# Gated MLP in seven-product units: GeLU of the chunk before issued behind a PSUM copy, and the opening's weight split, column sums and copies in another order

## The chip, the cores and the metric

The kernel runs on one core of one Trainium2 chip. The metric is the device time of one execution in microseconds, the median of several. TensorE (PE) multiplies, VectorE (DVE) and ScalarE (ACT) work elementwise, GpSimd (POOL) and SyncE (SP) here mostly issue DMAs. Each engine works through its own instructions in the order in which the kernel writes them and waits on semaphores for the others.

## What is computed

Two decoder layers on 512 tokens of 1024 channels. Each ends in the same gated MLP, and that is the part that the change touches:

```python
def conv_ffn(x, norm, w_up, dw_w, dw_b, w_down):
    h = rms_norm(x, norm) @ w_up                          # 1024 -> 2 * 3072
    g = causal_dwconv(h[..., :D_FF], dw_w, dw_b)          # width 3 over tokens
    u = h[..., D_FF:]
    return (jax.nn.gelu(g) * u) @ w_down                  # 3072 -> 1024
```

Around it, in both layers, stand a token mixer and a cross-attention, each with RMSNorm and a residual sum. All matrix products are made in three passes: each operand is split into a rounded high part and the rest, and `mm3` (lines 184 to 188) multiplies high by high, high by low and low by high into one PSUM bank. So each weight block needs a high part (an ACT copy) and a low part (a DVE subtraction).

## The kernel before

Activations lie with channels on the 128 partitions and tokens along the row. `ffn` (line 835) cuts the 3072 gate and 3072 value channels into 24 chunks of 128 each. Chunks 0 and 1 are plain: eight k-steps of 128x512 products. Chunks 2 to 23 are **units**: a 2 by 2 block product of half the k-range and half the tokens (256), done in seven products instead of eight, as in the schemes of Strassen and Winograd. The token side of the sums (`seven.T1` to `T4`) is made once for a layer by `Seven.sums`. The weight side (`Blocks`) is made for each unit: the raw blocks are loaded, `high` (line 798) copies a block on ACT (L815), `low` (line 820) subtracts on DVE (L822), and `low` of a11, s3 and s2 also issues accumulating DMAs on POOL's queue (L825, L828, L830), which turn the raw block into the next sum. The sums hang on each other: a11 must be split before s3 can be made, s3 before s1 and s2, and s2 before s4.

`unit(c)` (line 927) has three PSUM tiles of 128x256: G, F and H. G is the left half of the gate. F begins as a copy of the first product in G (L924 in `ahead`, which is called for the next unit before a unit ends) and then takes the products s2, s3 and a22. It is copied out after s2 (L941, into the left half of tile u) and after s3 (L955). s3 may not be added before L941 has read F. H takes s1 and s4. PE's order in a unit is: s1 into H, s2 into F, a12 into G, s3 into F; then the down projection, or in units 2 and 3 a plain chunk; then a11 of the next unit, s4 into H and a22 into F.

The down projection follows four chunks behind: unit c, from 4 on, has a `Down` that copies two 128x512 rows of the residual X into PSUM (`bank`, L854, ACT), adds 24 products of 128x512 onto each pair, and copies them home (L858).

The elementwise work on a finished unit is the generator `gating(c, ...)` (line 897). It is held in `left` and stepped by `next(left)` inside the following unit. Its steps in order: the token convolution (L891 on ACT, two taps L894 on DVE), the GeLU (L896, ACT), the product with the values (L910, DVE), the high part of the result (L913, ACT) and its low part (L915, DVE). In `unit` the GeLU step stands ahead of L941, L910 behind it, then the copy of the next unit's a22 (L815), then L913, and then the two `bank` copies.

`opening()` (line 1044) starts the MLP of a layer. PE makes the two products of plain chunk 0 (`start(0)` and `start(1)`, 24 products each) and in their midst `mean_of` (L287, L288), the column sums of squares. From these come the root (L1056), the loading of the GeLU table (L1057) and the reciprocal `norm.r` (L1059), with which chunk 0's gate is scaled (L1012). Then follow its convolution, GeLU and value (L891, L894, L896, L1015, L1018, L1020 on DVE and ACT), mixed with splits of weights for units 2 (`first`) and 3 (`second`) and with `ahead(first)`.

What sets the order: `tc.manual_schedule(engines=ORDERED)` keeps PE, ACT, DVE and POOL in the order of the code. SP's loads are placed by the scheduler, and they wait for free buffers; the raw weights have three.

## Time and profile before

| | |
|---|---|
| median of 3 runs | 1452.84 us (1452.17 to 1453.44) |
| the profiled execution | 1449.17 us, its span 1447.4 us |
| PE busy | 1423.2 us, 98% of the span |
| DVE, ACT busy | 1077.3 us (74%), 912.8 us (63%) |
| granted TensorE clock, mean | 0.996 |
| MLP units, layer 0 and layer 1 | first L941 at 380.0 us, last L941 at 1403.6 us, 44 in all |

The profiled execution is the one whose rows are quoted; it was 3.67 us below the median of the other three. A row of the timeline has the start in the span, the duration, the engine, the line and operation, the tile written and those read, the size, and in brackets how long the engine had idled before and which instruction ended that wait. Matmuls are pipelined, so their durations overlap: their cost is the distance between two starts. With PE at 98% nearly all that can be won or lost is in the places where PE's starts stand further apart than usual.

### The profile page before, as it was taken

What the parts mean: (1) busy time and instruction counts of PE and PEld (TensorE: products, weight loads), DVE (VectorE), ACT (ScalarE), POOL (GpSimd) and SP (SyncE); (2) the same over time, 40 slices, a digit from 0 to 9 for tenths busy, and PEclk for the clock granted to TensorE, in tenths of its full rate; (3) what the DMA queues carried; (4) which work ended last, traced back from release to release, by engine and by line L of the source; (5) the groups of instructions that cost most, each with busy time, mean ns of one, the idle gap of its engine ahead of it and who ended that gap; (6) DMA issues with size and microseconds to landing.
All of it is one profiled execution on the core that took longest, in us unless ns stands there. A gap on an engine that the chain in (4) does not pass through costs nothing.

```text
span 1447.4 us, 22826 instructions
## 1 busy us (share of the span) xinstructions
PE 1423.2 (98%) x8650; PEld 1265.9 (87%) x8650; DVE 1077.3 (74%) x1792; ACT 912.8 (63%) x1600; POOL 316.8 (22%) x333
## 2 busy tenths in 40 slices
PE   9999999999899999999999999999989999999998
PEld 8888888987799999999988777899869999999997
DVE  7987775769676676666788997877777676676665
ACT  7668754667466666666665547667655666666664
POOL 0012300100122222222008992011012222222211
PEclk9999999999999999999999999999999999999999
DMA  8522232543577777777442364345347777777751
GB/s 305 188 88 88 90 129 75 123 108 118 122 170 174 162 175 172 163 172 167 129 131 88 117 170 147 99 96 132 105 112 168 168 176 166 166 174 171 162 125 59
DMA packets 80030, 204.32 MB, mean 141 GB/s; under 512 B 9008, under 2 KB 9520, under 8 KB 79920
## 3 DMA queue, kind: packets, MB, share of 16 engines
q1 hardware_dynamic: 50832, 150.15, 33.7%
q0 software_dynamic: 28800, 52.44, 21.2%
q8 instruction: 67, 1.10, 0.3%
q14 instruction: 43, 0.35, 0.1%
q10 hardware_dynamic: 288, 0.27, 0.1%
HBM read 145.16 MB, written 2.10 MB: 102 GB/s over the span
## 4 chain that ended last, share of the span: by engine, by line
PE 84%; DVE 6%; issue 3%; ACT 2%; DMA 2%; POOL 2%; SPq 0%; POOLq 0%; DVEq 0%; ACTq 0%
PE mm L186 20%; PE mm L187 20%; PE mm L188 20%; PE aux L186 7%; PE aux L187 7%; PE aux L188 7%; PE mm L458 2%; DMA raw<-in_wv 1%; DVE wlo L167 1%; DMA raw<-raw 1%; POOL actf L1484 1%; DVE wlo L203 0%; PE aux L532 0%; ACT whi L166 0%; POOL act L167 0%
## 5 line engine op out<-in xcount | busy, mean ns | idle before, releaser
L187 PE MATMUL mm<-act,whi 128*128 128x512 f32 (+2 forms) x1029 | 357.7, 348 | 0.5 <-DVE act L181 0.4
L186 PE MATMUL mm<-act,whi 128*128 128x512 f32 (+2 forms) x1029 | 357.5, 348 | 0.0
L188 PE MATMUL mm<-act,wlo 128*128 128x512 f32 (+2 forms) x1029 | 357.3, 347 | 0.0
L187 PEld LDWEIGHTS mm<-act,whi 128*128 128x128 f32 x1029 | 195.3, 190 | 26.5 <-DVE act L167 1.0
L186 PEld LDWEIGHTS mm<-act,whi 128*128 128x128 f32 x1029 | 195.1, 190 | 26.5 <-ACT tmp L1483 0.8
L188 PEld LDWEIGHTS mm<-act,wlo 128*128 128x128 f32 x1029 | 195.3, 190 | 23.9 <-DVE wlo L167 0.6
L186 PE MATMUL mm<-bigr,bigr 128*128 128x256 f32 x704 | 201.1, 286 | 9.8 <-ACT tmp L941 6.6
L187 PE MATMUL mm<-bigr,bigr 128*128 128x256 f32 x704 | 200.3, 285 | 0.0
L188 PE MATMUL mm<-bigr,bigr 128*128 128x256 f32 x704 | 200.3, 285 | 0.0
L186 PE MATMUL aux<-act,whi 128*128 128x512 f32 x431 | 168.6, 391 | 0.0
L187 PE MATMUL aux<-act,whi 128*128 128x512 f32 x431 | 168.2, 390 | 0.0
L188 PE MATMUL aux<-act,wlo 128*128 128x512 f32 x431 | 167.7, 389 | 0.0
L166 ACT ACTIVATE whi<-raw 128x1024 fp32r<-128x1024 f32 (+1 forms) x95 | 96.5, 1020 | 84.7 <-PE mm L187 44.0
L828 POOL DMA_DIRECT2D raw<-wa x100 | 87.1, 890 | 284.6 <-DVE bigr L822 166.4
L186 PEld LDWEIGHTS mm<-bigr,bigr 128*128 128x128 f32 x704 | 136.2, 193 | 11.0 <-ACT tmp L941 7.4
L171 DVE TENSOR_TENSOR tmp<-mm,tmp 128x256 f32<-128x256 f32 x130 | 53.9, 419 | 121.2 <-PE mm L188 118.6
L815 ACT ACTIVATE bigr<-raw 128x512 fp32r<-128x512 f32 x176 | 109.0, 622 | 53.4 <-DVE wlo L203 42.2
L187 PEld LDWEIGHTS mm<-bigr,bigr 128*128 128x128 f32 x704 | 136.3, 194 | 0.0
L188 PEld LDWEIGHTS mm<-bigr,bigr 128*128 128x128 f32 x704 | 136.3, 194 | 0.0
L822 DVE TENSOR_TENSOR bigr<-raw,bigr 128x512 fp32r<-128x512 f32 x176 | 120.9, 688 | 13.4 <-ACT bigr L815 9.6
L825 POOL DMA_DIRECT2D raw<-raw x50 | 43.2, 865 | 399.4 <-DVE wlo L822 205.6
L167 DVE TENSOR_TENSOR wlo<-raw,whi 128x1024 fp32r<-128x1024 f32 (+1 forms) x75 | 90.3, 1209 | 21.0 <-ACT whi L166 20.7
(354 smaller groups left out, 3084.9 us busy)
## 6 DMA issues: line engine op xcount, KB each, us to landing
raw<-wa POOLq DMA_DIRECT2D x150, 256.0 KB, 3.9
wa<-in_wpair SPq DMA_DIRECT2D x88, 256.0 KB, 3.7
raw<-in_wpair SPq DMA_DIRECT2D x44, 512.0 KB, 3.8
big<-in_wdown SPq DMA_DIRECT2D x42, 512.0 KB, 4.0
raw<-raw POOLq DMA_DIRECT2D x50, 256.0 KB, 4.9
raw<-in_pw SPq DMA_DIRECT2D x24, 512.0 KB, 3.3
raw<-in_win SPq DMA_DIRECT2D x20, 512.0 KB, 3.3
raw<-in_wk SPq DMA_DIRECT2D x16, 512.0 KB, 3.4
```

Source lines behind the costliest of these rows:

```text
L166: A.activation(hi, src, AF.Copy)
L167: fetched[1] = (eng or V).tensor_tensor(lo, src, hi.bitcast(F32), op=ALU.subtract)
L171: V.tensor_tensor(out, a, b, op=ALU.add)
L186: PE.matmul(ps, wh, xh, start=first, stop=False, skip_group_check=onto)
L187: PE.matmul(ps, wh, xl, start=False, stop=False, skip_group_check=onto)
L188: PE.matmul(ps, wl, xh, start=False, stop=last, skip_group_check=onto)
L458: PE.matmul(p, m[j], x, start=k == 0 and j == 0 and x is hi, stop=k == C - 1 and x is lo)
L815: A.activation(self.w[name][0], self.block(name), AF.Copy)
L822: V.tensor_tensor(lo, self.block(name), hi.bitcast(F32), op=ALU.subtract)
L825: G.dma_start(self.r, self.z, accum_op=ALU.add)
L828: G.dma_start(block, self.a22, accum_op=ALU.add)
L1484: G.tensor_tensor(z[:, s:], z[:, s:], f[:, s:], op=ALU.add)
```

## The change

Two edits. In `unit`, the step that issues the GeLU of the chunk before now stands behind the copy L941. In `opening`, the column sums come later on PE (after all of `start(0)` and two k-steps of `start(1)`), block a11 of unit 3 is loaded and split ahead of the last sums of the norm, `ahead(first)` comes before the second and third step of chunk 0's gate, block s3 of unit 3 is split in the opening too (before, it was split in unit 2), and s4 of unit 2 one step later.

```diff
@@ unit
             m(c, F, "s2", seven.T2, False)
-            next(left, None)
             u, f, g = tmp_f(), tmp_f(), tmp_f()
             A.activation(u[:, :M], F, AF.Copy)
+            next(left, None)
             next(left, None)
             high(c + 1, "a22")
@@ opening
             ss = split(norm.ss)
-            start(0, range(6))
+            start(0)
+            start(1, range(2))
             mean = mean_of(ss)
-            start(0, range(6, C))
-            start(1)
+            start(1, range(2, C))
             Norm.due = None
+            pairs[second].load()
+            pairs[second].load_second()
+            both(second, "a11")
             for _ in seven.sums(3):
                 pass
...
             fetch(2)
-            pairs[second].load()
-            pairs[second].load_second()
             g = gate(0)
             next(g)
             w[-1].low()
-            both(first, "s4")
+            pairs[second + 1].load()
+            chains = ahead(first)
+            both(second, "s3")
             next(g)
             next(g)
-            both(second, "a11")
+            both(first, "s4")
             next(g, None)
-            pairs[second + 1].load()
-            chains = ahead(first)
             left = values(0)
```

On ACT, in a unit with a down projection (here unit 5 of layer 0), this stood in a row before. L896 is the GeLU, L941 the copy of F, L815 a weight block's high part, L913 the high part of the gated chunk, L854 the two bank copies:

```order
L891 ACTIVATE tmp_4212<-tmp_4074,par 128x512
L815 ACTIVATE bigr_4227<-raw_3971 128x512
L896 ACTIVATE tmp_4212<-tmp_4212 128x512
L941 ACTIVATE tmp_4248<-mm_4171 128x256
L815 ACTIVATE bigr_4253<-wa_4152 128x512
L913 ACTIVATE act_4267<-tmp_4212 128x512
L854 ACTIVATE aux_4270<-x 128x512
```

And now, where the copy has the line number 940:

```order
L891 ACTIVATE tmp_4212<-tmp_4073,par 128x512
L815 ACTIVATE bigr_4227<-raw_3971 128x512
L940 ACTIVATE tmp_4247<-mm_4171 128x256
L896 ACTIVATE tmp_4212<-tmp_4212 128x512
L815 ACTIVATE bigr_4253<-wa_4152 128x512
L913 ACTIVATE act_4267<-tmp_4212 128x512
L854 ACTIVATE aux_4270<-x 128x512
```

The GeLU moved behind the copy, which waits for PE's s2 products; L913 and L854 stay behind the GeLU.

On ACT in the opening of layer 0, from the split of a plain weight (L200) to the first L941, before. L815 here are: s4 of unit 2 (`raw_3040`), a11 of unit 3 (`whi` from `raw_3648`), s3 of unit 3 (`bigr` from `raw_3648`):

```order
L200 ACTIVATE whi_3645<-raw_3643 128x1024
L891 ACTIVATE tmp_3656<-tmp_3654,par 128x512
L815 ACTIVATE bigr_3659<-raw_3040 128x512
L896 ACTIVATE tmp_3656<-tmp_3656 128x512
L815 ACTIVATE whi_3665<-raw_3648 128x512
L924 ACTIVATE mm_3674<-mm_3673 128x256
L815 ACTIVATE bigr_3701<-raw_3648 128x512
L1020 ACTIVATE act_3704<-tmp_3656 128x512
L941 ACTIVATE tmp_3723<-mm_3674 128x256
```

And now; a11 of unit 3 is no longer among them, as it stands ahead of the root, right behind the split of the sums of squares:

```order
L200 ACTIVATE whi_3656<-raw_3654 128x1024
L891 ACTIVATE tmp_3661<-tmp_3659,par 128x512
L924 ACTIVATE mm_3667<-mm_3666 128x256
L815 ACTIVATE bigr_3681<-raw_3619 128x512
L896 ACTIVATE tmp_3661<-tmp_3661 128x512
L815 ACTIVATE bigr_3689<-raw_3040 128x512
L1020 ACTIVATE act_3707<-tmp_3661 128x512
L940 ACTIVATE tmp_3722<-mm_3667 128x256
```

L924 moved up by three places, s3 of unit 3 from behind L924 and the GeLU to between them; L1020 still stands ahead of the copy of F.

## The prediction

> **What bounds the kernel now.** I read the page first, and in it the busy times:

> ```profile
> PE 1423.2 (98%) x8650; PEld 1265.9 (87%) x8650; DVE 1077.3 (74%) x1792; ACT 912.8 (63%) x1600; POOL 316.8 (22%) x333
> ```

> PE is busy for 98% of the span, so the time lies in PE's starts, and any wait of PE is lost. Then the view of waits, for PE alone; its columns are the total, the times and the longest:

> ```profile
> PE mm L186 <- ACT tmp L941: 6.6, 4, 2.6
> PE stat L287 <- ACT act L166: 4.0, 2, 2.9
> PE mm L186 <- ACT mm L924: 3.2, 2, 2.4
> ```

> These three, all within the MLP, are what the change is aimed at: the column sums and the first copies of F in the two openings, and two later copies L941. They occur eight times in 44 units. So an ordinary unit has no wait on PE at all. The timeline of PE in the opening of layer 0:

> ```profile
> 358.43 0.39 PE L188 MATMUL mm<-act,wlo 128*128 128x512 f32 x1
> ...
> 359.89 0.51 PE L287 MATMUL stat<-act,ones 128*128 128x512 f32 x1 [1.07 <-ACT act L166]
> ...
> 370.55 0.28 PE L188 MATMUL mm<-bigr,bigr 128*128 128x256 f32 x1
> 373.23 0.58 PE L186 MATMUL mm<-bigr,bigr 128*128 128x256 f32 x1 [2.40 <-ACT mm L924]
> ...
> 377.57 0.28 PE L188 MATMUL mm<-act,wlo 128*128 128x256 f32 x1
> 380.37 0.58 PE L186 MATMUL mm<-bigr,bigr 128*128 128x256 f32 x1 [2.52 <-ACT tmp L941]
> ```

> The view of windows gives the granted clock behind a wait (its columns: length, PE busy, clock, DMA share, GB/s):

> ```profile
> 374.00:377.00 3.00, 3.00 (x18) 0.56 0.91 266
> 380.00:383.00 3.00, 2.63 (x12) 0.51 0.85 146
> 1077.00:1080.00 3.00, 2.69 (x17) 1.00 0.86 146
> ```

> After both long waits of layer 0 the clock fell to about half for some 3 us; after the third, in layer 1, it did not. At half rate for 3 us some 1.4 us of work is lost, so a wait of 2.5 us costs 2.7 to 4.1 us.

> **What a unit without waits looks like.** Unit 5 of layer 0, ACT, then DVE, then PE:

> ```profile
> 427.41 0.63 ACT L896 ACTIVATE tmp<-tmp 128x512 f32<-128x512 f32 x1 [1.14 <-DVE tmp L894]
> 428.33 0.38 ACT L941 ACTIVATE tmp<-mm 128x256 f32<-128x256 f32 x1 [0.28 <-PE mm L188]
> 428.61 0.62 ACT L815 ACTIVATE bigr<-wa 128x512 fp32r<-128x512 f32 x1
> 429.13 0.62 ACT L913 ACTIVATE act<-tmp 128x512 fp32r<-128x512 f32 x1
> 429.65 1.11 ACT L854 ACTIVATE aux<-x 128x512 f32<-128x512 f32 x2
> ```

> ```profile
> 428.07 0.69 DVE L910 SCALAR_TENSOR_TENSOR tmp<-tmp,tmp 128x512 f32<-128x512 f32 x1 [0.16 <-ACT tmp L896]
> ```

> ```profile
> 430.89 0.28 PE L188 MATMUL mm<-bigr,bigr 128*128 128x256 f32 x1
> 431.01 0.40 PE L186 MATMUL aux<-act,whi 128*128 128x512 f32 x1
> 431.24 0.40 PE L187 MATMUL aux<-act,whi 128*128 128x512 f32 x1
> ```

> So PE needs 0.12 us for a product 256 wide and 0.23 for one 512 wide. The row at 431.01 is the first product of the down projection, which adds onto the first L854. It comes 2.68 us after L941 started, without a wait. A single L854 takes 0.593 us (the view of that line; two in each of 40 units):

> ```profile
> L854 ACT ACTIVATE aux<-x x80: 580/593/597, 414.7 to 1405.2; 128x512 f32<-128x512 f32 x80
> ```

> So the bank is ready at 429.65 + 0.59 = 430.24, and 0.77 us are spare.

> **The change in a unit, step by step.** Today the GeLU starts 0.92 us before L941, while ACT would otherwise be waiting for PE. Moved behind, it cannot start before L941 has: the next ACT instruction follows L941 after 428.61 - 428.33 = 0.28. Everything behind the GeLU hangs on it: L910 starts 428.07 - 427.41 = 0.66 after it. What follows L910 when nothing else holds it up is seen in unit 4, where today's GeLU is late:

> ```profile
> 413.46 0.69 DVE L910 SCALAR_TENSOR_TENSOR tmp<-tmp,tmp 128x512 f32<-128x512 f32 x1 [0.16 <-ACT tmp L896]
> ```

> ```profile
> 414.18 0.63 ACT L913 ACTIVATE act<-tmp 128x512 fp32r<-128x512 f32 x1
> 414.72 1.10 ACT L854 ACTIVATE aux<-x 128x512 f32<-128x512 f32 x2
> ```

> ```profile
> 415.36 0.50 PE L186 MATMUL aux<-act,whi 128*128 128x512 f32 x1
> 415.69 0.39 PE L187 MATMUL aux<-act,whi 128*128 128x512 f32 x1
> ```

> L913 starts 0.72 after L910, L854 0.54 after L913, and PE 415.36 - 414.72 = 0.64 after L854. The copy of a22 (L815, spacing 0.52) fits in between. Sum from the start of L941: 0.28 + 0.66 + 0.72 + 0.54 + 0.64 = 2.84 us, where PE comes at 2.68. So PE waits 0.16 us in each unit for a bank that was ready 0.77 us early. To that comes the restart: in unit 4 the second product follows the first after 0.33 us instead of the usual 0.23, since the wait also holds up the weights. Cost: 0.16 + 0.10 = 0.26 us a unit. The sum is relative to L941, which waits for PE, so the next unit pays it again. L854 runs in 40 units; units 5 to 23 of two layers are 38: 38 x 0.26 = 9.9, say **10 us lost**. The other late things (L913 +0.88, thus the weight copies behind the banks) end before ACT's next idle stretch, the 1.14 us ahead of the GeLU, and cost nothing.

> [...]

> Unit 4 has its own case: there L941 is late behind the GeLU, and the move frees it. But the bank decides there too, and it hangs on a GeLU that waits for DVE, which carries plain chunk 1 at that time. L913 of the unit before is 0.88 later, and DVE hands this on if it has no idle time until then. I take 0.9 us lost in each layer, **1.8 us**; zero is the other end.

> **The change in the openings.** The two waits there hang on these ACT and DVE rows:

> ```profile
> 368.15 0.82 ACT L891 ACTIVATE tmp<-tmp,par 128x512 f32<-128x512 f32 x1 [1.85 <-DVE tmp L1012]
> ...
> 371.75 0.63 ACT L896 ACTIVATE tmp<-tmp 128x512 f32<-128x512 f32 x1 [2.26 <-DVE tmp L894]
> ...
> 372.81 0.36 ACT L924 ACTIVATE mm<-mm 128x256 f32<-128x256 f32 x1
> 378.90 0.63 ACT L815 ACTIVATE bigr<-raw 128x512 fp32r<-128x512 f32 x1 [5.72 <-DMA raw<-raw]
> ...
> 379.95 0.36 ACT L941 ACTIVATE tmp<-mm 128x256 f32<-128x256 f32 x1
> ```

> ```profile
> 363.92 3.35 DVE L1059 RECIPROCAL r<-tmp 128x512 f32<-128x512 f32 x1
> ...
> 370.13 1.53 DVE L894 SCALAR_TENSOR_TENSOR tmp<-tmp,par,tmp 128x511 f32<-128x511 f32 x2
> ...
> 374.33 0.69 DVE L1018 TENSOR_TENSOR tmp<-mm,tmp 128x512 f32<-128x512 f32 x1
> ```

> ```profile
> 373.93 0.86 POOL L825 DMA_DIRECT2D raw<-raw  x1 [28.30 <-DVE wlo L822]
> ```

> L825, released by the split of a11 of unit 3, took 5.0 us to land (373.93 to 378.90), and ACT stood before s3 with L941 behind it. With a11 split some 12 us earlier the landing is off the path. What is late next: a11's copy pushes the sums on ACT by one spacing, 0.52, so the reciprocal starts at 364.44 and L891 at 368.67. L924 follows before 369.5, and PE 0.42 after its start (372.81 to 373.23 today), at 369.9. PE itself arrives earlier: from 358.66 on, without a wait for the sums, 32 products of 0.23 and 24 of 0.12 end at 368.9. That is a wait of 1.0 us, like the one of 1.07 at 359.89. Then on the path: s3 of unit 3 on ACT until 370.3, its low part on DVE (0.69) until 371.0, the taps (1.53) until 372.5, the GeLU until 373.2, s4 until 373.7 and its low part until 374.4, L1015 and L1018 (0.69 each) until 375.8, L1020, and 0.52 behind its start L941 at 376.4, ending 376.8. PE, ready at 369.9 + 24 x 0.12 = 372.8, starts at 376.8: a wait of 4.0 us, longer than today's, but ended 3.5 us earlier than at 380.37. The halved clock follows in both. **Gain in layer 0: 3.5 us.** Beside the path, at nothing: on SP the load of unit 3 goes ahead of that of a plain weight, which isn't needed on ACT before the reciprocal; on POOL the accumulations of unit 3 (L825, twice L828) are issued earlier, with nothing queued behind them but those of the same unit; the load of the next plain weight waits for s4's later split, and is needed a plain chunk later.

> Layer 1 today:

> ```profile
> 1058.21 0.49 PE L287 MATMUL stat<-act,ones 128*128 128x512 f32 x1 [2.90 <-ACT act L166]
> ...
> 1077.31 0.39 PE L186 MATMUL mm<-bigr,bigr 128*128 128x256 f32 x1 [2.63 <-ACT tmp L941]
> ```

> ```profile
> 1062.23 3.35 DVE L1059 RECIPROCAL r<-tmp 128x512 f32<-128x512 f32 x1
> ```

> The wait for the sums shrinks to under 1 us, but that only brings PE sooner to the copies. By the same chain L941 ends 12.3 us after the reciprocal's start, 1062.75 + 12.3, so PE goes on at 1075.1 instead of 1077.3: 2.2 earlier. Here, though, the clock stayed full, and after a wait of 4 us I expect it halved for part of the next 3 us; I take 1.0 of the 1.4 us. **Gain in layer 1: 1.2 us** (0.8 to 2.2). [...]

> Between the layers the scheduler sets some DVE and PE instructions otherwise; PE hardly waits there, and I put it at nothing, within 0.5 us either way.

> **Sum.** -3.5 - 1.2 + 1.8 + 9.9 = +7.0 us on the profiled execution's 1449.17 us. The median of the runs is 1452.84, 3.67 above it; I carry the difference over: **1460 us**. A change of 0.2%, 2.9 us, is about what a measurement here can tell from none.

> **Rivals.** *Slack holds:* the chain from L941 to the bank comes out under 2.68 us, so no unit pays. It decides at 0.16 us, spread over five hand-overs, each read from one or two rows; against it speaks how little they vary (one L854 from 580 to 597 ns). Then only the openings count, 1452.84 - 4.7 = 1448 us, faster. 9%. *Restart hidden:* the weights of the first aux product are loaded during the wait, and the 38 units lose 0.16 each: 6.1 + 1.8 - 4.7 = +3.2, 1456 us; against it the two rows of unit 4. 12%. [...] *Openings give more:* if the chain behind the reciprocal does not hold up L941, today's losses at the copies (two waits with half clock, 2 x 4.1 us in layer 0) go altogether, 4 to 7 us more are won, and the units' loss is cancelled: 1453 us. Against it: L1020 precedes L941 in the new order. 7%. *Forecast:* 72%, 1457 to 1463. The order on ACT is the one the edit says, so that it does nothing is no case.

> The range, 1455.5 to 1463.5, takes in the second rival, and above the forecast a chain 0.05 us longer (+1.9) and a halved clock behind unit 4. Faster 9%, the same 7%, slower 84%.

> **What would show it.** Right: in units 5 to 23 the GeLU starts 0.28 after the copy, the first aux product has a wait on L854 and comes 2.84 after the copy, so that the copies of successive units stand 0.26 us further apart; in the openings the wait for the sums is gone, the one for L924 about 1 to 2 us, the one for the copy about 4. Wrong: aux products at 2.68 after the copy, or a copy in the opening before 374.

## The result and the profile after

The changed kernel takes 1459.12 us in the median of 4 runs (1457.0 to 1460.09), the kernel before 1452.51 us of 4 runs (1450.43 to 1453.44): a ratio of 1.0046, 95% interval 1.0028 to 1.0063. It is slower, by 6.6 us (0.5%). The profiled execution took 1457.0 us, its span is 1455.2 us, 7.8 above the 1447.4 of before. The page's busy times, after:

```profile
PE 1431.6 (98%) x8650; PEld 1267.3 (87%) x8650; DVE 1076.8 (74%) x1792; ACT 908.0 (62%) x1600; POOL 316.7 (22%) x333
```

The share is still 98%, and the number of matmuls is the same. "Busy" contains the time in which a matmul runs at half clock (in layer 1's opening PE is busy for 3.10 of 3.10 us at a clock of 0.50, below), so the loss has to be read from waits and from the distances between starts. The view of waits of PE, after (total, times, longest):

```profile
PE mm L186 <- ACT tmp L940: 7.8, 2, 3.9
PE aux L186 <- ACT aux L854: 3.4, 2, 1.7
PE mm L186 <- ACT mm L924: 2.5, 2, 1.7
```

The wait for the column sums (L287, 4.0 us before) is gone, the one for the copy of F is longer in both openings, and a new one stands there, for the bank copies L854. It has only two entries, the two units 4. The other 38 units wait too, but too briefly for this view; they show in the timeline. Unit 5 of layer 0, after, ACT, then DVE, then PE:

```profile
426.37 0.38 ACT L940 ACTIVATE tmp<-mm 128x256 f32<-128x256 f32 x1 [2.06 <-PE mm L188]
426.65 0.62 ACT L896 ACTIVATE tmp<-tmp 128x512 f32<-128x512 f32 x1
...
428.03 0.63 ACT L913 ACTIVATE act<-tmp 128x512 fp32r<-128x512 f32 x1 [0.24 <-DVE tmp L910]
428.57 1.10 ACT L854 ACTIVATE aux<-x 128x512 f32<-128x512 f32 x2
```

```profile
427.30 0.69 DVE L910 SCALAR_TENSOR_TENSOR tmp<-tmp,tmp 128x512 f32<-128x512 f32 x1 [1.34 <-ACT tmp L896]
```

```profile
428.93 0.28 PE L188 MATMUL mm<-bigr,bigr 128*128 128x256 f32 x1
429.20 0.50 PE L186 MATMUL aux<-act,whi 128*128 128x512 f32 x1
429.54 0.39 PE L187 MATMUL aux<-act,whi 128*128 128x512 f32 x1
```

The GeLU starts 0.28 us after the copy, L913 1.66, L854 2.20, and the first product of the down projection 2.83, where before it came at 2.68. After the last product of s3 it starts 0.27 us later instead of 0.12, and the product behind it 0.34 later instead of 0.23. The distance of the copies in successive units, from the view of that line over four units, after and then before:

```profile
L940 ACT ACTIVATE tmp<-mm x4: 383/384/384, 426.4 to 473.8; 128x256 f32<-128x256 f32 x4
```

```profile
L941 ACT ACTIVATE tmp<-mm x4: 383/384/384, 428.3 to 474.9; 128x256 f32<-128x256 f32 x4
```

Three units take 47.4 us instead of 46.6, so 15.80 against 15.53 for one.

The openings, PE after, layer 0 and then layer 1, and the windows that give the clock (length, then busy time and count of PE, weight load, DVE, ACT and POOL, then the granted clock, DMA share, GB/s):

```profile
370.27 0.39 PE L186 MATMUL mm<-bigr,bigr 128*128 128x256 f32 x1 [0.84 <-ACT mm L924]
377.29 0.39 PE L186 MATMUL mm<-bigr,bigr 128*128 128x256 f32 x1 [3.88 <-ACT tmp L940]
...
1070.87 0.39 PE L186 MATMUL mm<-bigr,bigr 128*128 128x256 f32 x1 [1.70 <-ACT mm L924]
1077.89 0.58 PE L186 MATMUL mm<-bigr,bigr 128*128 128x256 f32 x1 [3.88 <-ACT tmp L940]
```

```profile
377.30:381.30 4.00, 4.00 (x17) 3.62 (x18) 2.44 (x6) 1.94 (x5) 0.00 (x0) 0.57 0.67 246
...
1077.90:1081.00 3.10, 3.10 (x13) 3.05 (x14) 1.42 (x3) 0.60 (x2) 0.00 (x0) 0.50 0.76 268
```

Each layer now has one wait of 3.88 us with a halved clock behind it. Before, layer 0 had two of about 2.5 with one behind each, and layer 1 a wait of 2.9 at the sums, with a halved clock behind it that the prediction does not mention (0.50 from 1059.30 to 1062.71), and one of 2.6 at the copy, with none.

To add all this up, PE's loss was worked out from the starts of all matmuls of a trace: the distance from each start to the next, less the usual distance behind a matmul of that shape (the one that a third of them undercut), summed over a stretch; a distance belongs to the start at its end. It counts waits, restarts and half clock alike. The "opening" runs from 5 us ahead of the reciprocal to 2 us ahead of unit 4's copy. In us, each for the profiled execution of a kernel (the experiments' names are explained below):

| | opening, layer 0 | opening, layer 1 | units 4 | units 5 to 23, both layers | between the layers | all else | total |
|---|---|---|---|---|---|---|---|
| before | 10.2 | 9.3 | 2.3 | 0.5 | 1.1 | 23.6 | 46.9 |
| after | 6.9 | 7.6 | 4.0 | 10.4 | 1.9 | 24.0 | 54.7 |
| e1_opening_alone | 7.5 | 8.9 | 2.3 | 0.5 | 1.2 | 25.1 | 45.5 |
| e2_unit_alone | 10.9 | 11.0 | 4.0 | 10.4 | 2.5 | 26.9 | 65.7 |
| e3_banks_first | 6.9 | 9.0 | 0.0 | 0.8 | 5.8 | 25.0 | 47.5 |
| e4_banks_later | 8.2 | 8.4 | 5.0 | 30.8 | 3.4 | 25.5 | 81.4 |
| e5_both_mended | 3.7 | 3.9 | 0.0 | 0.5 | 5.9 | 24.8 | 38.7 |
| e6_sums_alone | 10.5 | 9.8 | 2.4 | 0.5 | 1.1 | 25.2 | 49.5 |
| e7_open_mended_old_unit | 3.6 | 3.9 | 3.9 | 0.5 | 1.2 | 25.7 | 38.7 |
| e8_old_from_unit5 | 3.7 | 3.8 | 0.0 | 0.5 | 1.4 | 24.6 | 34.0 |
| e9_old_in_last_unit | 3.3 | 3.8 | 0.0 | 0.5 | 1.2 | 25.1 | 33.9 |

From before to after: -3.3 - 1.7 + 1.7 + 9.9 + 0.8 + 0.4 = 7.8 us, the whole difference of the spans. One reservation for this table: before's profiled execution was 3.3 us faster than its median, after's 2.1; the other kernels' lie within 0.9 us of theirs. So medians are compared with medians, and the table says only where a profiled execution lost its time.

### The profile page after: what moved, and what is told of

It is laid out like the page before. It is cut to its first block, busy times and chain, and to the rows that moved or that the text cites. A ratio compares the mean times of both kernels' runs of the same rounds, so it can differ in the third digit from the quotient of the medians.

```text
span 1455.2 us, 22822 instructions
## 1 busy us (share of the span) xinstructions
PE 1431.6 (98%) x8650; PEld 1267.3 (87%) x8650; DVE 1076.8 (74%) x1792; ACT 908.0 (62%) x1600; POOL 316.7 (22%) x333
## 3 DMA queue, kind: packets, MB, share of 16 engines
q0 software_dynamic: 28800, 52.44, 20.8%
## 4 chain that ended last, share of the span: by engine, by line
PE 83%; DVE 8%; ACT 3%; POOL 2%; issue 2%; DMA 1%; SPq 0%; POOLq 0%; ACTq 0%; DVEq 0%
PE mm L186 19%; PE mm L187 19%; PE mm L188 19%; PE aux L186 8%; PE aux L187 7%; PE aux L188 7%; PE mm L458 2%; DVE wlo L167 1%; DVE wlo L203 1%; POOL act L167 1%; DVE bigr L767 1%; DVE tmp L894 1%; DVE bigr L822 1%; POOL actf L1485 1%; PE aux L532 0%
## 5 line engine op out<-in xcount | busy, mean ns | idle before, releaser
L187 PE MATMUL mm<-act,whi 128*128 128x512 f32 (+2 forms) x1029 | 356.9, 347 | 0.3 <-DVE act L181 0.2
L186 PE MATMUL mm<-act,whi 128*128 128x512 f32 (+2 forms) x1029 | 356.3, 348 | 0.7 <-ACT act L274 0.6
L188 PE MATMUL mm<-act,wlo 128*128 128x512 f32 (+2 forms) x1029 | 356.6, 347 | 0.0
L186 PEld LDWEIGHTS mm<-act,whi 128*128 128x128 f32 x1029 | 194.5, 189 | 27.3 <-ACT act L274 1.3
L187 PEld LDWEIGHTS mm<-act,whi 128*128 128x128 f32 x1029 | 194.7, 189 | 26.6 <-DVE act L167 1.0
L188 PEld LDWEIGHTS mm<-act,wlo 128*128 128x128 f32 x1029 | 194.7, 189 | 23.7 <-DVE wlo L167 0.6
L186 PE MATMUL mm<-bigr,bigr 128*128 128x256 f32 x704 | 200.7, 285 | 10.3 <-ACT tmp L940 7.8
L187 PE MATMUL mm<-bigr,bigr 128*128 128x256 f32 x704 | 200.1, 284 | 0.0
L188 PE MATMUL mm<-bigr,bigr 128*128 128x256 f32 x704 | 200.0, 284 | 0.0
L186 PE MATMUL aux<-act,whi 128*128 128x512 f32 x431 | 173.0, 401 | 3.4 <-ACT aux L854 3.4
L187 PE MATMUL aux<-act,whi 128*128 128x512 f32 x431 | 168.3, 391 | 0.0
L188 PE MATMUL aux<-act,wlo 128*128 128x512 f32 x431 | 168.1, 390 | 0.0
L166 ACT ACTIVATE whi<-raw 128x1024 fp32r<-128x1024 f32 (+1 forms) x95 | 96.4, 1020 | 87.4 <-PE mm L187 45.2
L828 POOL DMA_DIRECT2D raw<-wa x100 | 87.5, 894 | 272.8 <-DVE bigr L822 172.6
L186 PEld LDWEIGHTS mm<-bigr,bigr 128*128 128x128 f32 x704 | 135.9, 193 | 11.1 <-ACT tmp L940 8.2
L188 PEld LDWEIGHTS mm<-bigr,bigr 128*128 128x128 f32 x704 | 136.1, 193 | 0.0
L815 ACT ACTIVATE bigr<-raw 128x512 fp32r<-128x512 f32 x176 | 108.8, 620 | 43.7 <-DVE wlo L203 43.7
L187 PEld LDWEIGHTS mm<-bigr,bigr 128*128 128x128 f32 x704 | 136.0, 193 | 0.0
L825 POOL DMA_DIRECT2D raw<-raw x50 | 43.2, 864 | 417.5 <-DVE wlo L822 409.3
L822 DVE TENSOR_TENSOR bigr<-raw,bigr 128x512 fp32r<-128x512 f32 x176 | 121.0, 689 | 8.7 <-ACT bigr L815 4.9
L167 DVE TENSOR_TENSOR wlo<-raw,whi 128x1024 fp32r<-128x1024 f32 (+1 forms) x75 | 90.3, 1210 | 20.4 <-ACT whi L166 19.9
```

The costliest lines, as they stand in the source:

```text
L166: A.activation(hi, src, AF.Copy)
L167: fetched[1] = (eng or V).tensor_tensor(lo, src, hi.bitcast(F32), op=ALU.subtract)
L186: PE.matmul(ps, wh, xh, start=first, stop=False, skip_group_check=onto)
L187: PE.matmul(ps, wh, xl, start=False, stop=False, skip_group_check=onto)
L188: PE.matmul(ps, wl, xh, start=False, stop=last, skip_group_check=onto)
L815: A.activation(self.w[name][0], self.block(name), AF.Copy)
```

## The experiments

The theory: the units lose because the moved GeLU delays the two bank copies, which stand behind it on ACT, past the moment when PE needs the first bank (0.16 us of wait and 0.10 of restart in each); and the openings gain, but less than they could, because unit 2's copy of F (unit 2 is called the second unit in the expectations) stands behind all of chunk 0's elementwise work. Rivals: the loss lies in the opening's new order; the delay comes from elsewhere in the unit than the banks; the restart is hidden; the later sums alone make the opening's gain. The first four kernels shared one chip and its runs of before (median 1453.03 us of 15), the next four another set (1452.84 us of 17), the last one its own (1453.41 us of 7).

**e1_opening_alone.** The changed opening, with the units in the order of before:

```diff
             m(c, F, "s2", seven.T2, False)
+            next(left, None)
             u, f, g = tmp_f(), tmp_f(), tmp_f()
             A.activation(u[:, :M], F, AF.Copy)
             next(left, None)
-            next(left, None)
```

> The changed opening with the unit as before (GeLU ahead of the copy of F). Bank theory: the units lose nothing again, unit 4 keeps its old 1.1 us, and the openings keep what they won: PE's lost time there 14.3 us instead of 19.3, so about 5 us faster than before, 1447.5 us. Rival (the openings are what got slower, the units are neutral): slower than before, about 1459 us. Rival (the new opening wins nothing that lasts): 1452.5 us.

1446.88 us (1445.18 to 1449.84), ratio 0.9959, interval 0.9945 to 0.9973. The time is as expected. The openings of the profiled execution lost 16.4 us and not 14.3, as the half clock lasted 6.8 us in each (3.4 in the changed kernel). The opening by itself is a gain of 6.1 us, and no unit waits for a bank; for the copies of F there are four waits, the two of 3.9 us in the openings and the two short ones in units 4 that before has as well:

```profile
PE mm L186 <- ACT tmp L941: 9.2, 4, 3.9
```

**e2_unit_alone.** The opening of before, with the GeLU behind the copy in all units (the other half of the change).

> The moved GeLU alone, with the opening as before. Bank theory: 38 units at 0.265 us (wait 0.16, restart 0.11) and two units 4 at 0.83 us more than before: 11.7 us slower, 1464 us. Rival (restart hidden, only the bare wait counts): 6.0 + 1.7, 1460 us. Rival (units neutral): 1452.5 us.

1467.93 us (1467.64 to 1468.91), ratio 1.0103, interval 1.0089 to 1.0117: slower by 14.9 us, 3.2 more than the 11.7 expected. The units lose what they lose in the changed kernel (10.4 us, and 4.0 in units 4). What the expectation lacked has to be sought elsewhere. The list of waits:

```profile
PE mm L186 <- ACT tmp L940: 7.5, 2, 4.0
PE mm L186 <- ACT mm L924: 4.8, 2, 2.4
...
PE stat L298 <- DVE actf L1499: 1.9, 1, 1.9
```

The copies L924 and L940 are still late in the old opening (10.9 and 11.0 us lost there), and a wait of layer 1's norm (L298), which was 1.0 us before, is 1.9 and is followed by half clock (0.50 from 884.78 to 888.19). In each opening the half clock lasted 6.8 us. The wait for the norm is no part of the theory: the same wait was 1.8 in e7_open_mended_old_unit and 0.6 to 1.0 in the others, and what sets it was not tried. By medians, the halves add to -6.1 + 14.9 = +8.8 us; the whole change gave +6.6.

**e3_banks_first.** The changed kernel, with the bank copies ahead of the GeLU:

```diff
             A.activation(u[:, :M], F, AF.Copy)
+            if down:
+                d = [down.bank(i) for i in range(2)]
             next(left, None)
             next(left, None)
...
             next(left, None)
-            if down:
-                d = [down.bank(i) for i in range(2)]
             next(left, None)
```

> The changed kernel with the two bank copies put between the copy of F and the GeLU. Bank theory: no product of the down projection waits for its bank any more, neither in units 5 to 23 nor in unit 4 (1.97 us each); 14 us less than the changed kernel, 1445 us, which is 6 to 7 us less than before. Rival (the units lose by the later GeLU itself, through what hangs on it): the GeLU is now another 1.1 us later, so 1459 us or more.

1450.13 us (1447.64 to 1452.03), ratio 0.9981, interval 0.9972 to 0.999. The same GeLU, just as late and even 1.04 us later, costs nothing in the units once the banks don't stand behind it. Unit 6, ACT and PE:

```profile
440.53 0.38 ACT L940 ACTIVATE tmp<-mm 128x256 f32<-128x256 f32 x1 [0.84 <-PE mm L188]
440.81 1.11 ACT L854 ACTIVATE aux<-x 128x512 f32<-128x512 f32 x2
441.85 0.62 ACT L896 ACTIVATE tmp<-tmp 128x512 f32<-128x512 f32 x1
```

```profile
443.09 0.28 PE L188 MATMUL mm<-bigr,bigr 128*128 128x256 f32 x1
443.21 0.40 PE L186 MATMUL aux<-act,whi 128*128 128x512 f32 x1
443.44 0.40 PE L187 MATMUL aux<-act,whi 128*128 128x512 f32 x1
```

The aux product comes 2.68 us after the copy, 0.12 after the product ahead of it, and its follower 0.23 later: no wait and no restart. So the rival "elsewhere in the unit" falls. The time lies 5 us above the expectation, though, and the table names the place: 5.8 us between the layers instead of 1.9, and 9.0 instead of 7.6 in layer 1's opening, where the half clock lasted 6.8 us instead of 3.4. Between the layers PE now waits longer for the next layer's norm, and half clock follows (0.58 in the window from 750 to 754):

```profile
749.69 0.49 PE L186 MATMUL mm<-act,whi 128*128 128x512 f32 x1 [1.50 <-ACT act L274]
```

The last kernel below asks for the cause.

**e4_banks_later.** The dose the other way: the changed kernel, with one more weight copy (s4 of the unit, spacing 0.52 us) ahead of the bank copies:

```diff
             next(left, None)
+            high(c, "s4")
             if down:
                 d = [down.bank(i) for i in range(2)]
...
-            high(c, "s4")
```

> The changed kernel with one weight copy (s4, spacing 0.52 us on ACT) moved ahead of the bank copies: the suspected wait made longer by 0.52 us. Bank theory: each of 40 units loses 0.52 us more and the restart stays at 0.1 us; 20.8 us more than the changed kernel, 1480 us. Rival (the loss is of another kind, or the wait has slack left): between 1459 and 1465 us.

1484.05 us (1483.31 to 1485.14), ratio 1.0213, interval 1.0199 to 1.0227. The wait is now long enough for the view of waits to list it in every unit, and unit 6 shows it:

```profile
PE aux L186 <- ACT aux L854: 24.1, 40, 2.2
```

```profile
448.09 1.10 ACT L854 ACTIVATE aux<-x 128x512 f32<-128x512 f32 x2
```

```profile
448.72 0.50 PE L186 MATMUL aux<-act,whi 128*128 128x512 f32 x1 [0.52 <-ACT aux L854]
```

PE comes 0.63 us after the start of the bank copies, as in the changed kernel, and the units lose 30.8 - 10.4 = 20.4 us more, 0.54 in each of 38: the full 0.52 of the added copy. So the bank is the bound there, one to one. The units 4 lose 1.0 us more, 0.5 each, as expected. The time is 4 us above the expectation, and what that lacked stands elsewhere in the table: 1.5 us more between the layers than in the changed kernel, 2.1 in the openings, where the half clock lasted 6.8 us in each, and 1.5 in all else.

**e5_both_mended.** e3_banks_first, and in the opening chunk 0's taps, GeLU, products and value (L894, L896, L1015, L1018, L1020, L1022) are no longer issued ahead of unit 2 but stepped inside it, from the GeLU on behind its copy of F. The split of s4 of unit 2, which stood between these steps, moves with them, to its usual place in the unit:

```diff
             chains = ahead(first)
             both(second, "s3")
-            next(g)
-            next(g)
-            both(first, "s4")
-            next(g, None)
-            left = values(0)
+            left = rest(g)
+
+        def rest(g):
+            next(g)
+            yield
+            next(g)
+            yield
+            next(g, None)
+            v = values(0)
+            next(v)
+            yield
+            next(v, None)
+            yield
```

> The kernel with the bank copies first, and in the opening chunk 0's taps, its GeLU, its gating product and its two parts of the value no longer issued between the second unit's first product and its first copy, but stepped inside that unit. Theory (the 4 us that TensorE waits for that copy in each opening are the queue of chunk 0 ahead of it on ScalarE and VectorE): the L940 wait of 7.8 us for both layers goes, and with it the half clock behind it, 1.6 to 2.9 us in each layer by the five openings seen so far. From 1450.1 us that is 11 to 13 us off: 1438 us, from 1436 to 1441. Rival (the copy is late for its own sake, its product is late because of the norm's reciprocal and L924): the wait stays in a large part, 1446 to 1450 us. Second rival: chunk 0's late GeLU makes a later wait in units 2 to 4: 1442 to 1446 us, with a wait for L1015 to L1020 or L853 in the list of waits.

1441.3 us (1439.2 to 1443.79), ratio 0.9923, interval 0.9911 to 0.9936, 8.8 us below e3_banks_first. The waits for L940 are gone from PE's list, and with them the half clock in the openings; what is left of the openings is L924, twice in each layer (units 2 and 3):

```profile
PE mm L186 <- ACT mm L924: 4.3, 4, 1.7
```

```profile
372.67 0.39 ACT L940 ACTIVATE tmp<-mm 128x256 f32<-128x256 f32 x1 [1.30 <-PE mm L188]
```

The copy now waits for PE (it started at 376.87 in the changed kernel, 12.0 us behind the start of the reciprocal; here 7.2). So those 4 us were the queue of chunk 0 with the split of s4 in it, not the norm; how much the split alone was worth was not tried. The expectation's 11 to 13 us were too many by 2 to 4: the openings fell by 8.3 us in all, since 7.6 us stay there, among them new waits for L924 and L822 of unit 3.

**e6_sums_alone.** The kernel before, with one part of the change: the column sums behind `start(0)` and two k-steps of `start(1)`.

```diff
-            start(0, range(6))
+            start(0)
+            start(1, range(2))
             mean = mean_of(ss)
-            start(0, range(6, C))
-            start(1)
+            start(1, range(2, C))
```

> The kernel before with one part alone: the column sums behind six blocks' products instead of ahead of them. The waits at L924 and L941 end when ScalarE is through with chunk 0, which the sums feed by the reciprocal; PE reaches those two waits sooner by what it no longer waits at the sums. Theory (the sums wait only stood in for the later ones): the 1.2 and 2.9 us at the sums come back at L924 and L941 in all but what the shorter or longer half clock makes: 1450 to 1454 us, ratio 0.998 to 1.001. Rival (the sums are worth their own wait): 1.8 us in layer 0 and 5.2 us in layer 1 go, 1446 us. Third: the norm's chain is itself later, since the sums now stand behind products: slower, 1455 us or more.

1452.28 us (1448.73 to 1455.81), ratio 0.9997, interval 0.9987 to 1.0008: no difference, as expected. The wait at L287 is gone and stands in the next place:

```profile
PE mm L186 <- ACT mm L924: 9.4, 2, 5.1
PE mm L186 <- ACT tmp L941: 5.9, 4, 2.7
```

L924 had 3.2 us before; the 4.0 of the sums and some more came back there. So the rival "the later sums alone make the opening's gain" falls: the gain of e1_opening_alone needs the new order of ACT's and DVE's work. Which part of that order brings it (a11 of unit 3 split early, L924 moved up), and whether the later sums help once it is there, was not tried.

**e7_open_mended_old_unit.** The opening of e5_both_mended, with the units in the order of before.

> The changed opening with chunk 0 stepped inside the second unit, and the units in the order of the kernel before (chunk's GeLU ahead of the copy). Theory: 1446.9 us of the opening alone, less the L941 wait of about 4 us and the half clock of 2 us in each layer, plus up to 1 us in each layer since chunk 0's GeLU now stands ahead of the second unit's copy: 1437 us, from 1435 to 1439. Rival (GeLU waits for the taps and holds the copy for 2 us or more, so the clock halves again): 1441 to 1444 us.

1441.21 us (1440.15 to 1441.61), ratio 0.9919, interval 0.9906 to 0.9931. Expected was 1437 us; it is missed. The openings came out as meant (3.6 and 3.9 us lost), but the units 4 lose 3.9 us instead of 2.3, and the norm's wait L298 is 1.8 here:

```profile
PE mm L186 <- ACT tmp L941: 4.5, 6, 1.5
...
PE stat L298 <- DVE actf L1509: 1.8, 1, 1.8
```

The 1.5 is unit 4's copy, which in this order stands behind a GeLU that is late there; before it had waited 0.7 (L941's 6.6 us less the 2.52 and 2.63 of the openings, for two). So where the GeLU of the chunk before is late, as in unit 4, it should not hold up the copy, nor the banks (in the changed kernel they stood behind it, and the units 4 lost 4.0); in the steady units it may stay ahead of the copy. The next kernel tries that.

**e8_old_from_unit5.** Both orders, each where it pays: the opening of e5_both_mended; copy, then banks, then GeLU in units 2 to 4; the order of before from unit 5 on.

```diff
+            early = not down or c == GC
             u, f, g = tmp_f(), tmp_f(), tmp_f()
+            if not early:
+                next(left, None)
             A.activation(u[:, :M], F, AF.Copy)
-            next(left, None)
+            if down and early:
+                d = [down.bank(i) for i in range(2)]
+            if early:
+                next(left, None)
             next(left, None)
...
-            if down:
+            if down and not early:
                 d = [down.bank(i) for i in range(2)]
```

> The changed opening with chunk 0 stepped inside the second unit; copy ahead of GeLU and bank copies first in units without a down product and in the first unit that has one, and the order of the kernel before in all later ones. Theory: as the old order in all units, less the 0.9 to 1.2 us that the first unit with a down product waits in each layer in either kernel, and less what GeLU ahead of the copy costs in the second unit: 1435 us, from 1433 to 1438. Rival (the first unit with a down product waits for something else that comes out behind it, or the layers' border shifts as it did with the bank copies first, 3.8 us): 1438 to 1441 us.

1436.74 us (1436.35 to 1438.86), ratio 0.9892, interval 0.9879 to 0.9905: faster than both kernels, and as expected. Of PE's waits in the MLP only L924 and a short L822 in the openings are left:

```profile
PE mm L186 <- ACT mm L924: 4.3, 4, 1.7
...
PE mm L188 <- DVE bigr L822: 0.8, 1, 0.8
```

**e9_old_in_last_unit.** As e8_old_from_unit5, but `early = c < CF - 1`: banks first and GeLU behind the copy in all units but a layer's last, which keeps the order of before.

> The kernel with both parts mended (bank copies first, chunk 0 stepped inside the second unit), but the last unit of each layer in the order of the kernel before. Asked is where the 4.5 us come from that the kernel with both parts mended loses more between the layers than the one with the old order from the second down unit on (5.9 against 1.4 us). Theory (what counts is the order of the instructions in a layer's last unit, behind which the next layer's norm begins): the loss between the layers falls to 1.1 to 1.9 us and the time to 1437 us, from 1435.5 to 1438.5. Rival (the norm's place hangs on how far ScalarE and VectorE run behind in all units): it stays, 1440 to 1442 us.

1436.93 us (1436.39 to 1439.4), ratio 0.9896, interval 0.9879 to 0.9912, as expected. The 4.5 us that e5_both_mended loses more between the layers come from the order in the last unit alone: 1.2 us are left. Part of the 4.5 is the half clock that fell behind the wait (0.50 from 747.39 to 750.80 in e5_both_mended); e4_banks_later has the same wait of 1.5 us without it and loses 3.4 there. Which of that unit's instructions pushes the norm, and why the changed order pushes it, was not tried. A second thing follows: in units 5 to 22 the two orders cost the same if the banks come first (0.5 us here and in e8_old_from_unit5).

## Why the prediction was right

**The units, 0.26 us each.** The sum of five hand-overs, 2.84 us against 2.68, came out at 2.83 (429.20 - 426.37), and each hand-over as taken: 0.28, 0.65, 0.73, 0.54, 0.63. The bank decides, as e3_banks_first (nothing lost) and e4_banks_later (0.54 more for 0.52 later) show. The loss of 38 units is 10.4 - 0.5 = 9.9 us; forecast were 9.9. *Slack holds* and the thought that anything else in the unit is the bound are out.

**The restart, 0.10 us.** The second aux product comes 0.34 after the first, the usual distance is 0.23. *Restart hidden* is out, and the view of L854 after shows why, in its list of who waited for it:

```profile
  PEld aux L186: 11.4, 40
```

By this row the weight load of the first aux product itself waits for the bank copy, in all 40 units; it is not done ahead of the wait.

**Unit 4, 0.9 us a layer.** It was +0.85. The step was argued from L913 of the unit before, and the rows bear it out. In unit 3 the low part L915 on DVE waits for L913, before and then after; the copy of F there starts at 396.11 and 393.24:

```profile
397.56 0.69 DVE L915 TENSOR_TENSOR act<-tmp,act 128x512 fp32r<-128x512 f32 x1 [1.01 <-ACT act L913]
```

```profile
395.56 0.69 DVE L915 TENSOR_TENSOR act<-tmp,act 128x512 fp32r<-128x512 f32 x1 [0.70 <-ACT act L913]
```

So L915 comes 1.45 us behind the copy before and 2.32 after, 0.87 later. From it to unit 4's L910 DVE takes as long as before (15.90 and 15.91 us), and hands the 0.87 on to the taps, for which unit 4's GeLU waits:

```profile
410.80 0.63 ACT L896 ACTIVATE tmp<-tmp 128x512 f32<-128x512 f32 x1 [0.88 <-DVE tmp L894]
```

**The openings, -3.5 and -1.2 us.** They were -3.3 and -1.7 in the profiled execution. The chain behind the reciprocal was taken with 376.8 - 364.44 = 12.4 us to PE's restart, and it was 12.39 (377.29 - 364.90). The reciprocal stood 0.46 later in the trace than forecast, but so did PE, by 0.46, from ahead of the opening on. ACT's part of the chain in layer 0, and the start of the reciprocal on DVE:

```profile
373.03 0.63 ACT L896 ACTIVATE tmp<-tmp 128x512 f32<-128x512 f32 x1 [2.27 <-DVE tmp L894]
...
376.33 0.63 ACT L1020 ACTIVATE act<-tmp 128x512 fp32r<-128x512 f32 x1 [2.16 <-DVE tmp L1018]
376.87 0.36 ACT L940 ACTIVATE tmp<-mm 128x256 f32<-128x256 f32 x1
```

```profile
364.90 3.35 DVE L1062 RECIPROCAL r<-tmp 128x512 f32<-128x512 f32 x1
```

The copy goes on ACT right behind L1020, and L1020 waits for DVE: that is the 4 us wait as forecast, 3.88. Its cause was only argued then; e5_both_mended shows it. In layer 1 two sizes were off. Up to PE's restart the loss fell by 3.1 us where 2.2 were taken, and the halved clock behind it cost 1.4 us more than before where 1.0 was taken. Most of the first is that the norm's split of the squares (L166 on ACT) comes 2.74 us later than in the trace of before (1057.53 and 1060.27), but PE's products ahead of the opening 3.50: the norm lags 0.76 us less behind PE. That this is the time which PE had by then lost between the layers is likely by its size, and not shown. That the opening by itself was worth 6.1 us by medians (e1_opening_alone) and not 4.7 lies within what before's own profiled execution was faster than its median. That the shorter wait for the sums "only brings PE sooner to the copies" was tried in e6_sums_alone: 0.9997.

**Between the layers.** Put at nothing, within 0.5; it was +0.7 us, just outside. In the kernel with both parts mended it is the last unit's order that counts there (e9_old_in_last_unit); that it is the same here is likely, not tried. PE's wait in the changed kernel shows what comes late:

```profile
753.62 0.49 PE L186 MATMUL mm<-act,whi 128*128 128x512 f32 x1 [0.60 <-ACT act L274]
```

**Sum.** 1460 us were forecast on a median of 1452.84, +7.0; the medians differ by 6.6 and the spans by 7.8. The units, most of the sum, came out by their mechanism. That the total is so near has some luck in it: the small terms were off by up to 0.8 us in both directions, and how long the clock stays halved, on which they hang, changed from one kernel to the next (3.4 or 6.8 us).

## What to carry to other kernels

An instruction that is moved behind a wait takes along everything that stands behind it on its engine: look not at its own consumers but at the first thing in that queue which the bound engine needs, and add up the hand-overs to it; here 0.77 us of spare time fell to a delay of 0.88 (the bank copies start 2.20 us behind the copy of F instead of 1.32) in 38 units. The remedy was not to undo the move but to pull the thing that is needed (the bank copies) ahead of the thing that is moved, and to leave the old order in the last unit of a layer. A wait that is removed at the head of a chain (the sums) is worth nothing as long as the chain's end is set by another engine (e6_sums_alone, ratio 0.9997).

## What the runs showed of the hardware

```profile
369.80:373.22 3.42, 1.03 (x9) 1.00 0.70 208
373.22:376.63 3.41, 3.40 (x16) 0.50 0.97 308
...
1072.95:1076.36 3.41, 1.72 (x15) 1.00 0.63 153
1076.36:1079.78 3.42, 2.48 (x17) 1.00 0.68 116
```

PE idled 2.39 us in the one, and 1.69 and 0.94 in the two. That the place of a wait counts beside its length is the author's reading of these two; no run moved a wait to try it.

In e1_opening_alone PE was still waiting when the clock was halved, and was busy for only 1.48 us of the first 3.41; the half clock lasted 6.82 us:

```profile
376.05:379.46 3.41, 1.48 (x7) 0.50 0.78 291
379.46:382.87 3.41, 3.41 (x13) 0.50 0.33 96
```

In layer 1 of the changed kernel, where PE was busy for 3.10 us of the first 3.41 (from 1077.58), it lasted these 3.41.

What it costs can be read in layer 0 of the changed kernel: from 377.87 to 381.28 eight products 256 wide stand 0.21 us apart instead of 0.12, and four 512 wide 0.42 to 0.43 instead of 0.23, 1.53 us in all. This is of the order of the wait itself, and it differed between kernels with equal waits: layer 1's opening lost 7.6 us in the changed kernel, with 3.4 us of half clock behind the wait of 3.9, and 9.0 in e3_banks_first, with 6.8 us of it behind the same wait.
